# Moving the on-chip addresses of an encoder layer's tiles: large tiles to multiples of 1 KB, small tiles into two pools of their own

## The chip, the cores and the metric

The kernel runs on one core of one Trainium2 chip. The metric is the device time of one launch in microseconds (us), as the median of several runs. The engines are named as in the profile: PE is TensorE (PEld its weight load, the read of the stationary operand), DVE is VectorE, ACT is ScalarE, POOL is GpSimd, SP is SyncE. A tile is a piece of on-chip memory: 128 partitions, and in each partition a run of bytes that begins at the same address. When an address is given below, it is the byte address within a partition.

## The reference, cut to what matters

One encoder layer on 256 tokens of width 2048, everything in float32:

```
x = x + 0.5 * swiglu(rmsnorm(x, ffn1_norm), ffn1_w_gate, ffn1_w_up, ffn1_w_down)   # inner width 5632
h = rmsnorm(x, mix_norm)
proj  = h @ w_in                                    # pool | q | k | v | q_mem | three gates
gates = sigmoid(proj[..., c5:] + b_gate)
merged = gates_0 * (pooling_branch(u_pool, pool_w, pool_scale) @ w_up_pool)
       + gates_1 * (dilated_attention_branch(q, k, v, positions) @ w_up_attn)
       + gates_2 * (memory_branch(q_mem, rmsnorm(mem, mem_norm), w_mem_kv) @ w_up_mem)
x = x + merged @ w_out
x = x + 0.5 * swiglu(rmsnorm(x, ffn2_norm), ffn2_w_gate, ffn2_w_up, ffn2_w_down)
return rmsnorm(x, final_norm)
```

The weights are read once (the page counts 458 MB read from HBM), and nearly all the arithmetic is matrix products against them.

## The kernel before, in words

**Products.** Every float32 product is made of three float32r products: each operand is split into a high part (`wh`, `lhs[:, 0]`) and a low part (`wl`, `lhs[:, 1]`), and PE adds low times high, high times high and high times low (`gemm`, lines 495 to 522). The weights are the moving operand, 512 columns at a time; the activations are the stationary operand, 128 columns at a time. So a usual PE instruction streams 512 float32r numbers (2,048 bytes of each partition) from `wh`, `wl`, `sumsh` or `sumsl`, and has loaded 128 columns (512 bytes) from `lhs` or `seven`. The two feed-forward parts use a scheme of seven instead of eight block products for six of the eight row pairs (`pair_gemm`, lines 535 to 602).

**Path of a weight tile.** SP issues a 1 MB load of `wf`; ACT rounds it to `wh`; DVE subtracts to get `wl` (`split`, lines 424 to 431, called from `weights` and `pair_weights`); PE uses both. PE's results in PSUM are taken up by ACT and DVE (`finish`, lines 604 to 623). Where an activation has to be turned, PE does it with the 128 x 128 identity tile `ident` as an operand (`turn_steps`, lines 706 to 717).

**Tiles and pools.** All on-chip tiles come from one pool `sb`. Large ones share 23 places of 8 KB ("slot", line 395), 4 of 4 KB ("tmp", line 401) and 2 of 2 KB ("half", line 404). Small ones (`one`, `gains`, `small`, `rstd`, `ssq`, `pos_i`) take a few bytes, rounded up to 32, and `ident` takes 512 bytes. The pool lays its places one behind the other, in the order in which each is first used.

**Order.** The kernel first records all instructions, and a planner (`Plan`, lines 178 to 372) orders them by estimated durations and gives each tile one of its group's places. The planner knows places by number and not by address.

Of the kernel before, what the change touches and what calls it, by code (L numbers as in the profile page):

```python
# [9 lines left out]
F32 = mybir.dt.float32  # L10
F32R = mybir.dt.float32r
BF16 = mybir.dt.bfloat16
I32 = mybir.dt.int32
# [4 lines left out]
P = 128  # L18
S = 256
T = S // P  # L20
D = 2048
KB = D // P
DFF = 5632
CW = 512
NCH = D // CW
# [24 lines left out]
def turn_parts():  # L50

    from fractions import Fraction

    pi = Fraction(
        314159265358979323846264338327950288419716939937510582097494459230781640628620899,
        10 ** 80,
    )
    rest = 1 / (2 * pi)
    parts = []
    for bits in (14, 26, 38, 50, 62):  # L60
        n = int(rest * 2 ** bits)
        parts.append(float(n) / 2.0 ** bits)
        rest -= Fraction(n, 2 ** bits)
    return parts
# [317 lines left out]
@with_exitstack  # L382
def tile_encoder_layer(ctx: ExitStack, tc: tile.TileContext, a: dict, out: bass.AP):
    nc = Plan(tc)
    sb = nc.pool(ctx.enter_context(tc.tile_pool(name="sb", bufs=1)))
    ps = nc.pool(ctx.enter_context(tc.tile_pool(name="ps", bufs=1, space=bass.MemoryType.PSUM)))
    dr = nc.pool(ctx.enter_context(tc.tile_pool(name="dr", bufs=1, space=bass.MemoryType.DRAM)))
    count = [0]

    def nm(s):  # L390
        count[0] += 1
        return f"{s}{count[0]}"

    def slot(shape, dtype=F32, name="slot"):
        return sb.tile(shape, dtype, tag="slot", bufs=23, name=nm(name))
# [4 lines left out]
    def tmp(shape, name="tmp", dtype=F32):  # L400
        return sb.tile(shape, dtype, tag="tmp", bufs=4, name=nm(name))
# [2 lines left out]
        return sb.tile(shape, dtype, tag="half", bufs=2, name=nm(name))  # L404

    def small(shape, name="sm"):
        return sb.tile(shape, F32, tag="small", bufs=10, name=nm(name))

    def psum(i, shape, name="bank"):
        return ps.tile(shape, F32, tag=f"p{i}", bufs=1, name=nm(name))  # L410
# [212 lines left out]
                nc.scalar.activation(c, Q[q], AF.Copy)  # L623


    one = sb.tile([P, 1], F32, name="one")
    nc.vector.memset(one, 1.0)
    nc.scalar.activation(one, one, AF.Copy)

# [2 lines left out]
    idle_out = psum(7, [P, CW], "idle")  # L632
    for _ in range(WARM):
        nc.tensor.matmul(idle_out, idle_in[:, :P], idle_in, start=True, stop=True)
    gains = sb.tile([P, 4 * KB + 8], F32, name="gains")
    nc.sync.dma_start(out=gains, in_=a["gains"])
    g_ffn1, g_mix, g_mem, g_ffn2 = (gains[:, i * KB : (i + 1) * KB] for i in range(4))
    pool_scale = gains[:, 4 * KB :]

    ident = sb.tile([P, P], F32, name="ident")  # L640
    nc.gpsimd.memset(ident, 1.0)
    nc.gpsimd.affine_select(
        out=ident, in_=ident, pattern=[[-1, P]], base=0, channel_multiplier=1, compare_op=ALU.is_equal, fill=0.0
# [137 lines left out]
        nc.scalar.activation(junk, src, AF.Square, accum_out=ssq[:, t, n : n + 1])  # L781

    def rstd_tile(nt=T):
        return sb.tile([P, nt], F32, tag="rstd", bufs=4, name=nm("rstd"))

    def rstd_of(ssq, nt=T, r=None):

        if r is None:
            r = rstd_tile(nt)
        v, q = small([P, nt]), small([P, nt])  # L790
        nc.vector.reduce_sum(v, ssq, axis=AX.X)
        nc.vector.tensor_scalar(v, v, 1.0 / D, EPS, op0=ALU.mult, op1=ALU.add)
        nc.scalar.activation(q, v, AF.Sqrt)
        nc.vector.reciprocal(r, q)
        nc.vector.tensor_mul(q, r, r)
        nc.vector.tensor_mul(q, q, v)
        nc.vector.tensor_scalar(q, q, -0.5, 1.5, op0=ALU.mult, op1=ALU.add)
        nc.vector.tensor_mul(r, r, q)
        return r

    def late_rstd(ssq):
        r = rstd_tile()
        queue(lambda: rstd_of(ssq, r=r))
        return r

    def ssq_tile():
        return sb.tile([P, T, NCH], F32, tag="ssq", bufs=2, name=nm("ssq"))


    lhs1 = pair_tiles()  # L810
    ssq1 = ssq_tile()
    rstd1 = []
    xts = []
# [116 lines left out]

    def rope_pieces():
        freq = tmp([P, H], "freq")
        pos_i = sb.tile([P, T], I32, name="pos_i")
        pos = small([P, T], "pos")
        work = slot([P, 14, T * H], F32, "angle")
        hi_r = slot([P, T * H], F32R, "hi_r")
        whole = slot([P, 10, T * H], F32, "whole")
        ang, hi, lo, acc = work[:, 10], work[:, 11], work[:, 12], work[:, 13]
        prod = work[:, :10]

        def load():
            nc.sync.dma_start(out=freq, in_=a["freq"])
            nc.sync.dma_start(out=pos_i, in_=a["positions"])

        def angles():
            nc.vector.tensor_copy(pos, pos_i)
            for t in range(T):
                nc.vector.tensor_scalar(ang[:, t * H : (t + 1) * H], freq, pos[:, t : t + 1], None, op0=ALU.mult)
            nc.vector.tensor_copy(hi_r, ang)
            nc.vector.tensor_copy(hi, hi_r.bitcast(F32))  # L950
            nc.vector.tensor_sub(lo, ang, hi)
            for i, part in enumerate(turn_parts()):
                nc.vector.tensor_scalar(work[:, i], lo, part, None, op0=ALU.mult)
                nc.vector.tensor_scalar(work[:, 5 + i], hi, part, None, op0=ALU.mult)


        def within(m):
            nc.vector.tensor_scalar(whole, prod, m, -m, op0=ALU.add, op1=ALU.add)
            nc.vector.tensor_sub(prod, prod, whole)

        def wrap(x):
            nc.vector.tensor_scalar(whole[:, 0], x, ROUND, -ROUND, op0=ALU.add, op1=ALU.add)
            nc.vector.tensor_sub(x, x, whole[:, 0])

        def total():
            nc.vector.tensor_add(acc, work[:, 4], work[:, 9])
            wrap(acc)
            for i in (3, 8, 2, 7, 1, 6, 0, 5):
                nc.vector.tensor_add(acc, acc, work[:, i])
                wrap(acc)  # L970


        def tables():
            quarter = ang
            nc.vector.tensor_scalar_add(quarter, acc, 0.25)
            wrap(quarter)
            scale = float(np.float32(2 * np.pi))
            for t in range(T):
                c, s = quarter[:, t * H : (t + 1) * H], acc[:, t * H : (t + 1) * H]
                nc.scalar.activation(rope[:, t, 0, :H], c, AF.Sin, scale=scale)  # L980
                nc.scalar.activation(rope[:, t, 0, H:], c, AF.Sin, scale=scale)
                nc.scalar.activation(rope[:, t, 1, :H], s, AF.Sin, scale=-scale)
                nc.scalar.activation(rope[:, t, 1, H:], s, AF.Sin, scale=scale)

        return [load, angles, lambda: within(ROUND_FAR), lambda: within(ROUND), total, tables]
# [4 lines left out]
    def mem_pieces():  # L990

        ssq = ssq_tile()
        rows, columns = {}, {}

# [31 lines left out]

    lhs_mix = []
    ssq2 = ssq_tile()

    def after1(n, t, xs):  # L1030
# [31 lines left out]
    def mem_head(qT, kT, v, h, L):  # L1062
# [3 lines left out]
        def scores():  # L1066
            b = bank([P, T, S])
            for t in range(T):
                for db in range(2):
                    j = 2 * h + db  # L1070
                    for x, y in THREE:
                        nc.tensor.matmul(
                            b[:, t], qT[:, x, j, t * P : (t + 1) * P], kT[:, y, j],
                            start=db == 0 and x == 1, stop=db == 1 and y == 1,
                        )
            mx, den = small([P, T]), small([P, T])
            scale = 256 ** -0.5
            nc.vector.reduce_max(mx, b, axis=AX.X)
            nc.vector.tensor_scalar(mx, mx, -scale, None, op0=ALU.mult)
            p = half_tmp([P, T, S], F32, "pm")  # L1080
            for t in range(T):
                nc.scalar.activation(
                    p[:, t], b[:, t], AF.Exp, bias=mx[:, t : t + 1], scale=scale, accum_out=den[:, t : t + 1]
                )
            nc.vector.reciprocal(den, den)
            for t in range(T):
                nc.vector.tensor_scalar(p[:, t], p[:, t], den[:, t : t + 1], None, op0=ALU.mult)
            state["p"] = p
# [115 lines left out]
    def gated(i, n, lhs, w_up, first, beside=None):  # L1204
# [26 lines left out]
        queue(*(lambda t=t: merge(t) for t in range(T)), soon=True)  # L1231

    rope_work = rope_pieces()
    for n in range(NCH):
        for _ in range(2 if n < 3 else 0):
# [248 lines left out]
```

## Time and profile before

| | us |
|---|---|
| median of 3 runs (2306.33 to 2308.55) | 2307.55 |
| the profiled execution, its own time | 2307.88 |
| its span, first to last instruction in the trace | 2306.1 |
| PE busy | 2286.4 |
| DVE busy | 1871.0 |
| ACT busy | 1270.7 |

PE is busy for 99% of the span, and its granted clock is full (2.4 GHz) in nearly all of it. Since matmuls overlap each other in the pipeline, the busy time doesn't say how fast PE goes; the distance from one matmul's start to the next one's does. The feed-forward parts lie at about 0 to 760 us and 1600 to 2297 us, the branches between them. All program lines carry the helper's number L225, so groups are told apart by the names of the tiles.

### The profile page before, as it was taken

How to read it: one execution, taken by the hardware profiler on the slowest of the kernel's cores; microseconds unless marked ns; L12 is line 12 of the kernel's file. 1: busy time of each engine (PE TensorE's matmuls, PEld its weight loads, DVE VectorE, ACT ScalarE, POOL GpSimd, SP SyncE). 2: the span in 40 equal slices, each digit the busy share in tenths (PEclk: the TensorE clock that was granted, in tenths of full speed). 3: DMA queues.
4: the chain of work that ended last, by engine and by line, in shares of the span. 5: the costliest groups of instructions: out<-in, count | busy, mean ns of one | idle time of the engine just before them, and what ended most of it. 6: DMA issues, size and time to landing. Idle time of an engine off the chain costs nothing.

```text
span 2306.1 us, 26456 instructions
## 1 busy us (share of the span) xinstructions
PE 2286.4 (99%) x10211; PEld 1866.8 (81%) x10211; DVE 1871.0 (81%) x1805; ACT 1270.7 (55%) x1244; POOL 163.6 (7%) x221
## 2 busy tenths in 40 slices
PE   9999999999999999999999999999999999999998
PEld 6887888888887888888888888888888888888886
DVE  7999999999987675856677567876599999999995
ACT  8666666666666453633333554445466666666663
POOL 0011111111110000000000000000001111111110
PEclk9999999999999999999999999999999999999999
DMA  9578788877886453655455556656477878778893
GB/s 347 191 230 236 238 238 249 228 224 233 249 320 223 171 214 119 230 194 201 170 195 182 174 201 214 225 208 215 144 224 230 240 222 243 234 223 245 237 301 119
DMA packets 115822, 506.18 MB, mean 219 GB/s; under 512 B 13680, under 2 KB 13936, under 8 KB 84464
## 3 DMA queue, kind: packets, MB, share of 16 engines
q1 hardware_dynamic: 88416, 443.66, 54.8%
q0 software_dynamic: 26992, 59.78, 12.8%
q8 instruction: 80, 1.31, 0.2%
q10 hardware_dynamic: 288, 1.05, 0.1%
q14 instruction: 46, 0.38, 0.0%
HBM read 458.30 MB, written 46.14 MB: 219 GB/s over the span
## 4 chain that ended last, share of the span: by engine, by line
PE 56%; issue 35%; POOL 4%; DMA 2%; DVE 2%; ACT 1%; SPq 0%; POOLq 0%; DVEq 0%; ACTq 0%
PE acc L225 39%; PE q L225 12%; POOL x L225 4%; PE down L225 3%; PE bank L225 2%; DMA x<-y 1%; DVE wl L225 1%; DMA mem<-in_mem 1%; DMA wf<-in_ffn_w_up 0%; DMA xt<-in_memT 0%; ACT wh L225 0%; DVE sums L225 0%; DVE lhs L225 0%; SPq L225 0%; ACT junk L225 0%
## 5 line engine op out<-in xcount | busy, mean ns | idle before, releaser
L225 DVE TENSOR_TENSOR wl<-wf,wh 128x2048 fp32r<-128x2048 f32 (+2 forms) x419 | 885.0, 2126 | 162.3 <-ACT wh L225 121.3
L225 ACT ACTIVATE wh<-wf 128x2048 fp32r<-128x2048 f32 (+2 forms) x419 | 741.4, 1783 | 305.9 <-PE acc L225 108.8
L225 PE MATMUL acc<-wh,lhs 128*128 128x512 f32 x2688 | 842.0, 394 | 0.0
L225 PEld LDWEIGHTS acc<-wh,lhs 128*128 128x128 f32 x2688 | 498.0, 188 | 107.3
L225 PE MATMUL acc<-wl,lhs 128*128 128x512 f32 x1344 | 525.5, 392 | 0.4 <-DVE wl L225 0.4
L225 PE MATMUL down<-wh,lhs 128*128 128x512 f32 x1152 | 359.2, 391 | 0.0
L225 PE MATMUL q<-wh,seven 128*128 128x512 f32 x972 | 303.4, 393 | 4.0 <-DVE lhs L225 2.0
L225 ACT ACTIVATE sumsh<-sums 128x1024 fp32r<-128x1024 f32 x228 | 237.1, 1057 | 117.2 <-DVE sums L225 117.2
L225 PEld LDWEIGHTS acc<-wl,lhs 128*128 128x128 f32 x1344 | 252.6, 188 | 56.0 <-DVE wl L225 1.1
L225 PE MATMUL q<-sumsh,seven 128*128 128x512 f32 x912 | 274.5, 391 | 0.0
L225 DVE TENSOR_TENSOR sumsl<-sums,sumsh 128x2048 fp32r<-128x2048 f32 x114 | 260.5, 2285 | 15.3 <-ACT sumsh L225 15.0
L225 PEld LDWEIGHTS down<-wh,lhs 128*128 128x128 f32 x1152 | 216.3, 188 | 47.6
L225 PE MATMUL q<-wh,lhs 128*128 128x512 f32 x704 | 232.2, 411 | 1.0 <-ACT wh L225 1.0
L225 ACT ACTIVATE y<-down 128x512 f32<-128x512 f32 x144 | 86.4, 600 | 254.8 <-PE down L225 141.8
L225 PE MATMUL down<-wl,lhs 128*128 128x512 f32 x576 | 225.4, 391 | 0.0
L225 PEld LDWEIGHTS q<-wh,seven 128*128 128x128 f32 x972 | 182.3, 189 | 46.3 <-PE q L225 4.8
L225 POOL DMA_DIRECT2D x<-y x144 | 123.9, 860 | 1133.1 <-ACT y L225 1126.1
L225 PEld LDWEIGHTS q<-sumsh,seven 128*128 128x128 f32 x912 | 171.2, 188 | 37.4
L225 PE MATMUL q<-wl,seven 128*128 128x512 f32 x486 | 190.0, 392 | 0.0
L225 DVE TENSOR_TENSOR sums<-sums,wf 128x512 f32<-128x512 f32 x228 | 157.8, 692 | 7.7
L225 PE MATMUL q<-sumsl,seven 128*128 128x512 f32 x456 | 163.6, 391 | 0.0
L225 PEld LDWEIGHTS q<-wh,lhs 128*128 128x128 f32 x704 | 120.2, 189 | 32.4 <-ACT wh L225 2.5
(137 smaller groups left out, 1603.9 us busy)
## 6 DMA issues: line engine op xcount, KB each, us to landing
wf<-in_w_in SPq DMA_DIRECT2D x100, 1024.0 KB, 4.9
wf<-in_ffn_w_down SPq DMA_DIRECT2D x88, 1024.0 KB, 7.1
wf<-in_ffn_w_gate SPq DMA_DIRECT2D x175, 512.0 KB, 5.2
wf<-in_ffn_w_up SPq DMA_DIRECT2D x175, 512.0 KB, 6.7
x<-y POOLq DMA_DIRECT2D x144, 256.0 KB, 6.4
wf<-in_w_mem_kv SPq DMA_DIRECT2D x16, 1024.0 KB, 4.9
wf<-in_w_out SPq DMA_DIRECT2D x16, 1024.0 KB, 4.9
wf<-in_w_up_pool SPq DMA_DIRECT2D x8, 1024.0 KB, 4.8
```

The lines of the kernel that those rows point to most:

```text
L225: return getattr(getattr(self.nc, engine), name)(*map(real, args), **{k: real(v) for k, v in kw.items()})
```

## The change

The program that is built before and after has the same 16,160 instructions in the same order on each engine, with the same waits. What differs is where tiles lie. The small tiles go to a pool `sm` that is laid ahead of the large tiles, `ident` to a pool `end` behind them, and `one` is made 64 bytes long, which makes `sm` 896 bytes; together with 128 bytes of constants that precede it, the large tiles then begin at 17,408 = 17 x 1,024. The places behind it are 8, 4 and 2 KB long, so that all of them begin at multiples of 1 KB.

The addresses, as the allocator's table in each built program has them:

| tiles | before | mod 1,024 (mod 64) | after | mod 1,024 (mod 64) |
|---|---|---|---|---|
| 21 of the 23 slots, the 1st tmp place | 17,344 to 185,280 | 960 (0) | 17,408 to 185,344 | 0 (0) |
| the 2 half places | 193,504 and 195,552 | 992 (32) | 193,536 and 195,584 | 0 (0) |
| the other 2 slots | 197,600 and 205,792 | 992 (32) | 197,632 and 205,824 | 0 (0) |
| the other 3 tmp places | 213,984 to 222,176 | 992 (32) | 214,016 to 222,208 | 0 (0) |
| `rope` | 226,752 | 448 (0) | 226,304 | 0 (0) |
| `ident` | 16,544 | 160 (32) | 228,352 | 0 (0) |
| small tiles | 16,512; 17,056; 193,472; 226,272 to 226,720; 228,800 | multiples of 32 | 16,512 to 17,376 | multiples of 32 |

Before, a 32-byte small tile (`ssq`, at 193,472) lies between the slots and the half places, which is why all that follows it stands 32 bytes off the rest. Within a tile, PE's operands begin at multiples of 512 bytes, so the remainders of the table hold for them too.

```diff
-    sb = nc.pool(ctx.enter_context(tc.tile_pool(name="sb", bufs=1)))
+
+    sm = nc.pool(ctx.enter_context(tc.tile_pool(name="sm", bufs=1)))
+    sb = nc.pool(ctx.enter_context(tc.tile_pool(name="sb", bufs=1)))
+    end = nc.pool(ctx.enter_context(tc.tile_pool(name="end", bufs=1)))
...
     def small(shape, name="sm"):
-        return sb.tile(shape, F32, tag="small", bufs=10, name=nm(name))
+        return sm.tile(shape, F32, tag="small", bufs=10, name=nm(name))
...
-    one = sb.tile([P, 1], F32, name="one")
+    one = sm.tile([P, 16], F32, name="one")[:, :1]
...
-    gains = sb.tile([P, 4 * KB + 8], F32, name="gains")
+    gains = sm.tile([P, 4 * KB + 8], F32, name="gains")
...
-    ident = sb.tile([P, P], F32, name="ident")
+    ident = end.tile([P, P], F32, name="ident")
...
-        return sb.tile([P, nt], F32, tag="rstd", bufs=4, name=nm("rstd"))
+        return sm.tile([P, nt], F32, tag="rstd", bufs=4, name=nm("rstd"))
...
-        return sb.tile([P, T, NCH], F32, tag="ssq", bufs=2, name=nm("ssq"))
+        return sm.tile([P, T, NCH], F32, tag="ssq", bufs=2, name=nm("ssq"))
...
-        pos_i = sb.tile([P, T], I32, name="pos_i")
+        pos_i = sm.tile([P, T], I32, name="pos_i")
```

## Rows read from the trace of the kernel before

**Rows 1.** The page: busy us (share of span) and instructions by engine.

```profile
PE 2286.4 (99%) x10211; PEld 1866.8 (81%) x10211; DVE 1871.0 (81%) x1805; ACT 1270.7 (55%) x1244; POOL 163.6 (7%) x221
PEclk9999999999999999999999999999999999999999
```

**Rows 2.** The waits of PE: waiter <- releaser, us in total, times, longest.

```profile
PE q L225 <- ACT wh L225: 2.9, 3, 2.0
PE bank L225 <- DVE lhs L225: 2.7, 1, 2.7
PE q L225 <- DVE lhs L225: 2.0, 5, 0.8
```

**Rows 3.** Groups by shape, DVE and ACT: count | busy us, mean ns | idle before.

```profile
L225 DVE TENSOR_TENSOR wl<-wf,wh 128x2048 fp32r<-128x2048 f32 x301 | 685.8, 2287 | 158.8 <-ACT wh L225 117.9 <-PE acc L225 32.7 <-issue 7.1
L225 ACT ACTIVATE wh<-wf 128x2048 fp32r<-128x2048 f32 x301 | 573.6, 1912 | 280.4 <-PE acc L225 108.8 <-DMA wf<-in_w_in 91.5 <-DVE wl L225 19.9
```

**Rows 4.** Stretches: start:end length, busy by engine (count), clock, DMA share, GB/s.

```profile
1089.61:1095.05 5.44, 5.44 (x26) 4.50 (x24) 4.05 (x2) 2.55 (x2) 0.00 (x0) 1.00 0.63 193
1095.73:1101.33 5.60, 5.60 (x25) 4.50 (x24) 5.44 (x13) 1.38 (x2) 0.00 (x0) 1.00 0.83 310
1542.58:1548.02 5.44, 5.44 (x26) 4.37 (x25) 1.23 (x5) 2.91 (x4) 0.00 (x0) 1.00 0.00 0
1548.02:1553.62 5.60, 5.60 (x26) 4.51 (x24) 3.69 (x3) 2.48 (x2) 0.00 (x0) 1.00 0.55 189
934.65:937.37 2.72, 2.72 (x14) 2.25 (x12) 2.72 (x2) 2.72 (x2) 0.00 (x0) 1.00 0.44 69
937.37:940.15 2.78, 2.78 (x14) 2.25 (x12) 2.78 (x2) 2.76 (x3) 0.00 (x0) 1.00 0.77 318
940.15:942.93 2.78, 2.78 (x14) 2.25 (x12) 2.78 (x3) 0.73 (x1) 0.00 (x0) 1.00 0.04 15
942.93:945.65 2.72, 2.72 (x14) 2.25 (x12) 2.69 (x4) 2.37 (x3) 0.24 (x1) 1.00 0.80 250
```

**Rows 5.** PE in order of time: start us, length, instruction, count [idle before].

```profile
349.78 0.39 PE L225 MATMUL q<-wl,lhs 128*128 128x512 f32 x1
350.94 0.70 PE L225 MATMUL q<-wh,seven 128*128 128x512 f32 x2 [0.77 <-DVE lhs L225]
351.48 0.40 PE L225 MATMUL q<-wl,seven 128*128 128x512 f32 x1
351.71 0.62 PE L225 MATMUL q<-sumsh,seven 128*128 128x512 f32 x2
352.40 0.62 PE L225 MATMUL q<-sumsh,seven 128*128 128x512 f32 x2
353.10 0.62 PE L225 MATMUL q<-sumsh,seven 128*128 128x512 f32 x2
353.78 0.62 PE L225 MATMUL down<-wh,lhs 128*128 128x512 f32 x2
...
354.46 0.62 PE L225 MATMUL down<-wh,lhs 128*128 128x512 f32 x2
```

**Rows 6.** DVE ahead of the wait in rows 5, same columns.

```profile
335.52 0.69 DVE L225 TENSOR_TENSOR v<-q,gate 128x512 f32<-128x512 f32 x1 [3.75 <-DMA x<-y]
...
347.31 2.28 DVE L225 TENSOR_TENSOR wl<-wf,wh 128x2048 fp32r<-128x2048 f32 x1
...
350.11 0.68 DVE L225 TENSOR_TENSOR lhs<-bank,lhs 128x512 fp32r<-128x512 f32 x1
```

**Rows 7.** Stretches as in rows 4: the two feed-forward parts without their ends.

```profile
60.00:760.00 700.00, 695.81 (x3086) 565.79 (x3085) 639.05 (x554) 436.36 (x442) 73.91 (x94) 1.00 0.77 238
1640.00:2200.00 560.00, 559.42 (x2480) 456.10 (x2479) 514.78 (x421) 344.53 (x326) 55.90 (x65) 1.00 0.76 226
```

**Rows 8.** PE where the stretch from 937.37 (rows 4) ends, columns of rows 5.

```profile
939.70 0.61 PE L225 MATMUL acc<-wh,lhs 128*128 128x512 f32 x2
940.15 0.40 PE L225 MATMUL acc<-wl,lhs 128*128 128x512 f32 x1
```

## The prediction

> **What bounds the kernel now.** I read the page first: PE is busy 2286.4 of 2306.1 us at a full granted clock [rows 1]. The list of PE's waits then says who holds it up: nobody for long. The three longest waits that come from other engines add up to 7.6 us, over 9 occasions [rows 2]. So the time is the number of PE's instructions times the distance from one start to the next. The program has 10,211 matmuls as the trace counts them, 9,642 of which stream 512 columns of float32r. If an address matters, it must show as a longer distance, or it must shorten what feeds PE.
>
> The program and the trace have the same number of matmuls in the same order, so each start in the trace can be laid beside the addresses of its operands in the built program. Before the change 21 of 23 slots lie at multiples of 64 bytes, and two lie 32 bytes off such a multiple, together with three tmp places, the half places and `ident`. That gives two kinds of operand to compare within one execution: "on" (address divisible by 64) and "off" (32 over).
>
> **What the rows show.** Four pairs of neighbouring stretches do it [rows 4]. (a) From 1089.61 us on, 24 matmuls with both operands on take 5.44 us, which is 226.7 ns each. From 1095.73 on, the next 24 stream a weight tile that lies at 205,792 (off), and take 5.60 us, or 233.3 ns each. (b) In the product with w_out, the 24 matmuls up to 1548.02 have both operands on: 5.44 us. The 24 from there on have their stationary operand in the tile at 205,792 (off), and the moving one on: 5.60 us. (c) From 937.37 on only every third matmul (the one with `wl`) is off. Blocks of 12 take 2.72, then 2.78, 2.78, then 2.72 us as the off tile comes and goes. In the third of these blocks the DMA engines are at 4% and in the fourth at 80%, so it isn't the traffic. DVE's and ACT's instructions show nothing of the kind: the 301 long `wl` subtractions average 2,287 ns and the 301 roundings 1,912 ns [rows 3], and told apart by on and off, in classes of 27 and more, their medians lie within 1 ns of each other for DVE and within 4 ns for ACT.
>
> There is a second way to a longer distance, which the change doesn't touch. After any break PE needs some ten matmuls to fall back into its step. After the wait that ends at 350.94, on operands that are all on, the threes that start at 351.71, 352.40 and 353.10 take 0.69, 0.70 and 0.68 us, and from 353.78 on 0.68 [rows 5]. The same happens after each group of turns with `ident`.
>
> The Trainium skill has a rule that speaks against all this: "SBUF — State Buffer", section Specifications, gives lines of 16 bytes, with a cost for crossing lines. A start 32 bytes over is a whole number of such lines, so by that rule on and off cost the same and the sum below is nothing. The trace doesn't agree: 5.44 against 5.60 us [rows 4].
>
> **The change, part by part.** *Moving the off tiles to multiples of 64.* In the program 1,570 of the 9,642 wide matmuls read at least one off operand (1,186 the moving one, 376 the stationary one, 8 both). Two prices follow from the rows. In a run of 24 each costs 0.16 us / 24 = 7 ns. In the pattern of every third, a block with 4 costs 0.06 us, or 15 ns each, since its neighbours are slowed too. So the price of all is between 1,570 x 7 = 11 and 1,570 x 15 = 24 us. Laid out one by one, the 9,343 wide matmuls with a distance under 260 ns fall into four kinds. 3,976 are far (over 12 matmuls) from any off operand, turn or break: they average 226.7 ns, as in the 5.44 us of [rows 4]. 3,812 are within 12 behind an off operand alone: 230.5 ns, together 14.6 us over the step of 226.7. 986 are within 12 behind a break or a turn alone: 3.4 us over. 569 are behind both: 2.8 us over, of which 569 x 3.5 ns = 2.0 would be there for the break alone. What goes with the off operands is 14.6 + 0.8 = 15.4 us, inside the bounds of 11 and 24.
>
> *Moving the on tiles* from 960 to 0 mod 1,024. No row shows an operand of PE at a multiple of 128, so this is bounded. From above: it could be as bad as off, 8,072 x 6.6 ns = 53 us. From below: the step of 226.7 ns is at 2.4 GHz 544 cycles for 512 columns; if all of the excess went, 13.4 ns x 9,642 = 129 us. I take nothing, the value of the nearest rows: all that is known to matter is the remainder by 64, and that stays 0; the distances between on tiles stay the same as well.
>
> *Moving `ident`* from off to on. The 3.4 + 2.0 us behind breaks and turns could go with it if the turns lose their step because `ident` is off. I take 0 of it, since a plain wait leaves the same trail with no `ident` in sight [rows 5]. As a bound it is -5 us.
>
> *Small tiles, half places, tmp places:* read and written by DVE and ACT, whose times show no address [rows 3], and off PE's path: nothing. *DMA:* the rows that loads write now start at multiples of 1 KB. The engines are at 77% and 76% in the feed-forward parts [rows 7], so a few per cent either way stay hidden behind PE.
>
> *What is late next.* DVE is the nearest: 639 of 700 us, 91%, in the first feed-forward part [rows 7]. Most of the time it runs ahead and waits. But at each chunk's end (63 us apart, some 20 in all) it is tied to PE: it takes up PSUM banks from 335.52 on, works without a break, and frees at 350.79 the bank for which PE waits 0.77 us [rows 5, 6]. In those 15 us DVE's work is fixed, so what PE saves there, 15 us x 0.7% = 0.1 us, comes back as a longer wait. For the 5 boundaries that wait already [rows 2] that is 0.5 us; if all 20 came to wait, 2 us. I take 1.2.
>
> *Sum:* -15.4 + 1.2 = -14.2 us. The profiled execution took 2307.88 us, 0.3 more than the median of 2307.55. From the median: 2293.3 us, 0.6% faster.
>
> **The rivals.**
> *R1, the slowness isn't of the remainder.* The two off slots are also the two highest, at 197,600 and 205,792, above 192 KB (196,608), and no PE operand of 512 columns lies high and on, or low and off. If the height is what slows PE, the change doesn't do what it says, since they stay high (197,632 and 205,824): 2307.5 us. For it: the rows can't part the two. Against it: with one off matmul in three, the 11th and 12th matmul of a block (939.70 to 940.15) are back at 0.45 us for two while the tile is still in use [rows 8], which looks like two streams running in and out of phase, not like a slower memory. By the rule of 16-byte lines the time would be the same.
> *R2, a finer remainder matters too, to the good.* Then the on tiles gain as well. One ns on each of 8,072 is 8 us; if the 544 cycles came half-way to 512, PE would save 65 us, and DVE at 91% would stop it at some 5%. For it: nothing is known of 0 mod 128. Against it: one step for all 21 on slots, whatever shares the memory with them. Time: about 2250 us.
> *R3, slower through the loads.* All loads now write rows that start at the same remainder of 1 KB. If that made the packets of one load meet in the same place of the memory, DMA time would grow. PE feels it only when the share passes 1, that is from 1 / 0.77 = 1.30 times the present time on. At 1.33 times, the 1,260 us of the two feed-forward parts would grow by 2.4%: +30 us, 2323 us with the gain above counted. Against it: before, 22 large places already shared one remainder (960).
>
> **How the numbers follow.** The forecast has 80%: 15.4 us from a count over one execution whose instructions stay the same, with a known cost for the two kinds of matmul. Within it the time goes from 2307.5 - 15.4 - 5 = 2287 (with the trails behind turns) to 2307.5 - 11 + 2 = 2299. R1 has 11%, R2 5%, R3 4%. The forecast's own range of 2287 to 2299 covers eight in ten, and nothing need be added. A measurement of this kernel can tell about 0.2% (4.6 us, the line at 2302.9) from no change. All of the forecast and R2 lie under it: 85% faster; R1 is 11% the same; R3 is 4% slower.
>
> **What would show it.** In the profile after, the long `wl` group of DVE stays at 2,287 ns. Runs of 24 wide matmuls take 5.44 us everywhere, also in the stretches that answer to 1095.73, 1548.02 and 937.37 [rows 4]; the trail behind waits stays. PE's waits for `lhs` from DVE grow by 1 or 2 us. If those stretches still take 5.60 us, the height of the two slots is the cause (R1). If the clean stretches fall below 5.44, it is R2. If PE's waits for `wh` grow by tens of us with loads that land later, it is R3.

## The result

The changed kernel takes 2290.9 us (median of 4 runs, 2290.32 to 2293.08) against 2307.86 us before. The ratio is 0.9929, with a 95% interval of 0.9912 to 0.9946. The forecast was 2293.3 us, in a range of 2287 to 2299. The time came as forecast, but the property that the prediction named as the cause, the remainder by 64, is not the cause. The experiments below found the one that is.

The page of the kernel after, the lines that answer to [rows 1]:

```profile
PE 2267.9 (99%) x10211; PEld 1865.5 (81%) x10211; DVE 1870.2 (82%) x1805; ACT 1270.1 (55%) x1244; POOL 163.4 (7%) x221
PEclk9999999999999999999999999999999999999999
```

PE lost 18.5 us of busy time with the same number of instructions; DVE and ACT lost less than 1 us each. The stretches of the kernel after that answer to those of [rows 4] (start:end, length, busy by engine with counts, granted clock, DMA share, GB/s):

```profile
1079.63:1085.08 5.45, 5.45 (x26) 4.51 (x25) 4.20 (x2) 2.79 (x2) 0.00 (x0) 1.00 0.59 192
1085.76:1091.19 5.43, 5.43 (x25) 4.50 (x24) 5.27 (x13) 1.03 (x2) 0.00 (x0) 1.00 0.82 305
1535.87:1541.31 5.44, 5.44 (x25) 4.51 (x24) 3.66 (x3) 2.47 (x2) 0.00 (x0) 1.00 0.54 194
928.45:931.17 2.72, 2.72 (x14) 2.25 (x12) 2.72 (x2) 2.70 (x3) 0.00 (x0) 1.00 0.89 355
931.17:933.89 2.72, 2.72 (x14) 2.25 (x12) 2.72 (x3) 0.81 (x1) 0.00 (x0) 1.00 0.03 12
```

The second and third rows are the same 24 matmuls each that took 5.60 us before, and the last two are the blocks of 12 that took 2.78. They now go at the pace of the undisturbed ones, 226.7 ns a matmul. The two highest slots are still the highest (197,632 and 205,824), and the second and third rows read them, so the rival R1 (height) falls here already. The waits of PE after, against [rows 2]:

```profile
PE q L225 <- DVE lhs L225: 3.4, 6, 1.0
PE q L225 <- ACT wh L225: 3.2, 3, 1.9
PE bank L225 <- DVE lhs L225: 2.6, 1, 2.6
```

PE's waits for `lhs` from DVE grew from 2.0 to 3.4 us.

**Where the 16.7 us between the two profiled executions lie** (spans of 2306.1 and 2289.4 us, matmuls laid side by side one for one; a distance is that from a matmul's start to the next one's):

| | before | after | difference |
|---|---|---|---|
| wide matmuls with a distance under 260 ns, their time over 226.7 ns each | 20.9 | 5.9 | -15.0 |
| breaks (260 ns and more), their time over 226.7 ns | 36.9 | 35.5 | -1.4 |
| ... of it, matmuls at half clock behind the first 5.5 us | 3.2 | 0.2 | -3.0 |
| ... of it, the rest, PE's waits for others among it | 33.7 | 35.3 | +1.6 |
| other matmuls, start and end | 62.8 | 62.5 | -0.3 |

The line of the half clock isn't the change's doing. In the profiled execution before, the granted clock fell to the lower level (1.2 of 2.4 GHz) for 16 matmuls behind two long waits, which cost 3 us. A second profile of the same kernel (label before_again) doesn't have it. The first 60 us and 15 us around the longest wait, of the kernel before:

```profile
0.00:60.00 60.00, 55.78 (x224) 42.25 (x225) 43.11 (x73) 48.73 (x77) 5.17 (x14) 0.97 0.87 334
690.00:705.00 15.00, 12.30 (x51) 9.56 (x51) 8.24 (x19) 11.68 (x27) 3.26 (x6) 0.89 0.96 374
```

and of its second profile:

```profile
0.00:60.00 60.00, 55.84 (x232) 42.69 (x232) 44.87 (x74) 50.49 (x78) 5.14 (x14) 1.00 0.88 334
690.00:705.00 15.00, 12.50 (x60) 9.90 (x59) 9.18 (x22) 12.03 (x28) 3.31 (x7) 1.00 0.88 341
```

The clock (0.97 and 0.89 against 1.00) and the count of matmuls (224 and 51 against 232 and 60) show it. That execution took 2304.2 us. The slower matmuls are in both profiles in the same size: 20.9 us over the step of 226.7 ns in each. So 13 to 15 us are the change's, and up to 3 us depend on which executions are compared.

### The profile page after: what moved, and what is told of

The parts are those of the page before. It is cut to its first block, busy times and chain, and to the rows that moved or that the text cites. A ratio compares the mean times of both kernels' runs of the same rounds, so it can differ in the third digit from the quotient of the medians.

```text
span 2289.4 us, 26456 instructions
## 1 busy us (share of the span) xinstructions
PE 2267.9 (99%) x10211; PEld 1865.5 (81%) x10211; DVE 1870.2 (82%) x1805; ACT 1270.1 (55%) x1244; POOL 163.4 (7%) x221
## 4 chain that ended last, share of the span: by engine, by line
PE 56%; issue 35%; POOL 4%; DMA 2%; DVE 2%; ACT 1%; SPq 0%; POOLq 0%; DVEq 0%; ACTq 0%
PE acc L225 39%; PE q L225 12%; POOL x L225 4%; PE down L225 3%; PE bank L225 2%; DMA x<-y 1%; DVE wl L225 1%; DMA mem<-in_mem 1%; DMA wf<-in_ffn_w_up 0%; DMA xt<-in_memT 0%; ACT wh L225 0%; DVE sums L225 0%; DVE lhs L225 0%; SPq L225 0%; ACT junk L225 0%
```

## The experiments

In what follows a "difference" is the start address of the moving operand less that of the stationary one. Each run's own time is compared with runs of the kernel before on the same chip.

**1. Only the high tiles put on (ssq64).**

```diff
-        return sb.tile([P, T, NCH], F32, tag="ssq", bufs=2, name=nm("ssq"))
+        return sb.tile([P, 2 * T, NCH], F32, tag="ssq", bufs=2, name=nm("ssq"))[:, :T]
```

> The kernel before with one edit: the small tile that lay between the slots takes 64 bytes instead of 32. All 21 on slots, the small tiles and ident stay where they were, at 960 mod 1,024 (ident 32 over a multiple of 64); the two high slots, the half and tmp places move by 32 bytes to multiples of 64. All 9,642 wide matmuls then read on operands. Theory (the remainder by 64 decides): about 2291 us, the whole gain of the change, with runs of 24 matmuls at 5.44 us everywhere. Rival R1 (the height of the two slots): 2307.5 us, nothing gained. Rival R2 (a finer remainder, such as 128 or 1,024, gave part of the gain): between 2293 and 2307 us.

Measured: 2309.7 us, ratio 1.0014 (1.0005 to 1.0024). So it is not faster but a trace slower. The theory and R2 are off; R1's "nothing gained" comes close, but R1 had fallen with the result. Every wide matmul reads operands at multiples of 64 here, so the remainder by 64 is not what matters. The stretches that answer to the first four of [rows 4], the clean one before the third left out:

```profile
1092.61:1098.05 5.44, 5.44 (x25) 4.50 (x24) 4.02 (x2) 2.80 (x2) 0.00 (x0) 1.00 0.51 193
1098.73:1104.24 5.51, 5.51 (x25) 4.51 (x24) 5.35 (x13) 0.98 (x2) 0.00 (x0) 1.00 0.81 302
1551.23:1556.83 5.60, 5.60 (x25) 4.51 (x24) 3.69 (x3) 2.49 (x2) 0.00 (x0) 1.00 0.53 189
```

In the second the weight tile lies at 0 mod 1,024 and the stationary one at 960: both at multiples of 64, with a difference of 64, and still slow. In the third the difference is -64, and the time is the 5.60 us of before.

**2. Two low tiles put off (low_off).** The places of the pool get a pad ahead of the seventh slot and one behind the eighth:

```diff
+                    key, pad = f"{tag or name}_{place}", lambda n: real.tile([P, 8], F32, tag=n, bufs=1, name=n)
+                    if key == "slot_6" and "before" not in pads:
+                        pads["before"] = pad("pad_before")
...
+                    if key == "slot_7" and "behind" not in pads:
+                        pads["behind"] = pad("pad_behind")
```

> The changed kernel with two 32-byte pads around two low slots, at 66,592 and 74,784, so that these two alone lie 32 bytes off a multiple of 64, and the two high slots (above 192 KB) are on. 1,575 wide matmuls read an off operand, against 1,570 in the kernel before. Theory (remainder by 64): the slowness comes back, 2291 + 15 to 16 = about 2306 us. Rival R1 (height of the slots): 2291 us or less than before by as much, since no high slot changes its kind from the changed kernel in a way that matters to it; if it was the height together with the remainder, also 2291 us.

Measured: 2324.99 us, ratio 1.0076 (1.006 to 1.0093), slower than any expectation. The pads move all that lies behind them too, so there are three kinds of slot: six at 0 mod 1,024, two at 32 and fifteen at 64. Only 4,487 of the 9,642 wide matmuls have a difference of 0 mod 256, against 8,080 before. The two stretches of 24 that answer to 1089.61 and 1095.73 of [rows 4]:

```profile
1095.91:1101.49 5.58, 5.58 (x25) 4.51 (x24) 3.94 (x2) 3.25 (x2) 0.00 (x0) 1.00 0.52 188
1102.19:1107.64 5.45, 5.45 (x25) 4.50 (x24) 5.29 (x13) 0.57 (x1) 0.00 (x0) 1.00 0.81 299
```

They have changed places. The first reads, in 14 of its 24 matmuls, a weight tile at 33,792 (0 mod 64) against a stationary one at 115,776 (0 mod 64), with a difference of 192 mod 256, and is slow. The second reads the high weight tiles at 205,888 and 197,696 against 107,584, with a difference of 0, and is fast. So high tiles are fast here and low ones slow: the height of the two slots isn't the cause.

**3. All large tiles put off (all_off).**

```diff
-    one = sm.tile([P, 16], F32, name="one")[:, :1]
+    one = sm.tile([P, 24], F32, name="one")[:, :1]
```

> The changed kernel with the first small tile 32 bytes longer, so that every large tile lies 32 bytes off a multiple of 64. All 9,642 wide matmuls read both operands off. Theory (each off operand costs by itself): 6.6 ns on each, 64 us, so about 2355 us, and more if two off operands cost more than one. Rival (only the difference between the remainders of the moving and the stationary operand costs, and these are equal here): 2291 us. Rival R1 (height): 2291 us.

Measured: 2293.48 us, ratio 0.9942 (0.9927 to 0.9957). With every wide matmul off in both operands, the kernel is as fast as the changed one. The rival named there, that only the difference costs, is the one that holds. The answers to [rows 4]:

```profile
1081.54:1086.98 5.44, 5.44 (x26) 4.50 (x24) 4.19 (x2) 2.64 (x2) 0.00 (x0) 1.00 0.60 193
1087.66:1093.10 5.44, 5.44 (x26) 4.50 (x24) 5.28 (x13) 1.09 (x2) 0.00 (x0) 1.00 0.83 304
1537.77:1543.21 5.44, 5.44 (x26) 4.50 (x24) 3.67 (x3) 2.48 (x2) 0.00 (x0) 1.00 0.56 194
```

**4. Matmuls alone (steps).** Two resident tiles that begin at multiples of 1 KB; each run of 36 reads them at chosen offsets:

```
for i in range(36):
    w = so + (i % 2) * 512 bytes
    matmul(bank, still[:, w : w + 128], moving[:, mo : mo + 512], ...)
```

> A kernel of its own with nothing but matmuls on two resident tiles that begin at multiples of 1 KB; it computes nothing of the reference and writes a copy of x. Runs of 36 matmuls, 512 columns of float32r, with the start of the moving and of the stationary operand moved by a chosen number of bytes: (0,0), (32,0), (0,32), (32,32), (64,0), (0,64), (64,64), (128,0), (256,0), (16,0), (0,16), (16,16), (48,0), (0,48), (8,0), (4,0), (0,4), (4,4), with (0,0) between the groups; then four runs with 256 columns, and seven with bf16. Theory (remainder by 64): 226.7 ns a matmul at 0, 64, 128 and 256; 233 ns at 32 of either operand; 4 to 48 slow as well, nothing said on how much. Rival (difference of remainders): (32,32), (16,16) and (4,4) at 226.7 ns. Rival R2 (finer remainders): (64,0), (0,64) or (128,0) slower than (0,0). bf16: open, no theory speaks of it.

24 matmuls out of each run; in order, the offsets (moving, stationary) in bytes are (0,0), (32,0), (0,32), (32,32), (64,0), (0,64), (64,64), (128,0), (256,0), (16,16), (4,4), then 512 columns of bf16 at (0,0) and (32,0):

```profile
27.18:32.62 5.44, 5.44 (x25) 4.50 (x24) 0.00 (x0) 0.00 (x0) 0.00 (x0) 1.00 0.02 3
35.41:41.01 5.60, 5.60 (x25) 4.50 (x24) 0.00 (x0) 0.00 (x0) 0.00 (x0) 1.00 0.00 0
43.81:49.41 5.60, 5.60 (x26) 4.51 (x24) 0.00 (x0) 0.00 (x0) 0.00 (x0) 1.00 0.00 0
52.16:57.60 5.44, 5.44 (x25) 4.50 (x24) 0.00 (x0) 0.00 (x0) 0.00 (x0) 1.00 0.00 0
68.56:74.05 5.49, 5.49 (x25) 4.51 (x24) 0.00 (x0) 0.00 (x0) 0.00 (x0) 1.00 0.00 0
76.84:82.44 5.60, 5.60 (x25) 4.49 (x24) 0.00 (x0) 0.00 (x0) 0.00 (x0) 1.00 0.00 0
85.19:90.63 5.44, 5.44 (x25) 4.51 (x24) 0.00 (x0) 0.00 (x0) 0.00 (x0) 1.00 0.01 3
93.41:98.97 5.56, 5.56 (x25) 4.51 (x24) 0.00 (x0) 0.00 (x0) 0.00 (x0) 1.00 0.00 0
101.76:107.20 5.44, 5.44 (x25) 4.50 (x24) 0.00 (x0) 0.00 (x0) 0.00 (x0) 1.00 0.00 0
134.85:140.37 5.52, 5.52 (x25) 4.50 (x24) 0.00 (x0) 0.00 (x0) 0.00 (x0) 1.00 0.00 0
193.46:199.17 5.71, 5.71 (x26) 4.54 (x24) 0.00 (x0) 0.00 (x0) 0.00 (x0) 1.00 0.00 0
227.13:232.31 5.18, 5.18 (x25) 2.35 (x24) 0.00 (x0) 0.00 (x0) 0.00 (x0) 1.00 0.00 0
234.90:240.08 5.18, 5.18 (x25) 2.35 (x24) 0.00 (x0) 0.00 (x0) 0.00 (x0) 1.00 0.00 0
```

No other engine works and next to nothing is moved by DMA (at most 3 GB/s), and the two paces of [rows 4] are there to the digit. (32,32) and (64,64) are as fast as (0,0), and (32,0), (0,32), (64,0), (0,64) and (128,0) are slow. The price belongs to a difference, and 256 is free again. The difference has a sign: (0,64) is -64, which is 192 mod 256, and takes 5.60 us, while (64,0) takes 5.49. Below 32 bytes the start itself counts as well: (16,16) takes 5.52 us and (4,4) 5.71, both with a difference of 0. With bf16 no offset that was tried changes anything.

**5. The period inside the kernel (low_256).** Like experiment 2, with the first pad alone, of 256 bytes in place of 32.

> The changed kernel with one pad of 256 bytes ahead of the seventh slot, so that six slots lie at 0 mod 1,024 and 17 at 256. 4,174 of the 9,642 wide matmuls then read operands that differ by 256 mod 512, the others operands that differ by 0. After the first four runs the theory is that the difference of the two operands' starts costs, by its remainder, and that 256 is as good as 0 (the matmul kernel showed 226.67 ns at 256): about 2291 us. Rival (only a common remainder by 1,024, or by 512, is free): 4,174 matmuls at up to 6.6 ns and their neighbours, 2310 to 2330 us.

Measured: 2291.88 us, ratio 0.9933 (0.9918 to 0.9948). Six slots at 0 and seventeen at 256 mod 1,024 cost nothing; a difference of 256 is as good as 0 in the kernel too.

**6. The period and the price of each difference (steps_fine).**

> The kernel of matmuls alone again, with the moving operand's start moved by 32 to 512 bytes in steps of 32, then the stationary operand's by 32 to 256, then both at 0 with the two stationary blocks that take turns 0, 512, 1,024, 256, 128, 64 and 32 bytes apart, then 256 columns with the moving operand moved by 0 to 256 in steps of 32. It computes nothing of the reference. Theory (difference mod 256): 226.7 ns at 0, 256 and 512, over 228 at all others, the same at d and d + 256; two stationary blocks 64 apart disturb like a difference of 64. If some difference lies under 226.7 ns, a faster layout than both kernels exists. If 288 and 32 differ, the period is longer than 256.

18 matmuls out of each run, with the moving operand moved by 32, 64, 96, 128, 160, 192, 224, 256 and 288 bytes, then with both at 0 and the two stationary blocks 256, 128 and 64 bytes apart:

```profile
27.30:31.50 4.20, 4.20 (x19) 3.37 (x18) 0.00 (x0) 0.00 (x0) 0.00 (x0) 1.00 0.01 4
34.26:38.38 4.12, 4.12 (x20) 3.38 (x19) 0.00 (x0) 0.00 (x0) 0.00 (x0) 1.00 0.00 0
41.18:45.38 4.20, 4.20 (x20) 3.38 (x18) 0.00 (x0) 0.00 (x0) 0.00 (x0) 1.00 0.00 0
48.18:52.38 4.20, 4.20 (x19) 3.38 (x18) 0.00 (x0) 0.00 (x0) 0.00 (x0) 1.00 0.00 0
55.19:59.41 4.22, 4.22 (x20) 3.39 (x19) 0.00 (x0) 0.00 (x0) 0.00 (x0) 1.00 0.02 4
62.21:66.41 4.20, 4.20 (x20) 3.37 (x18) 0.00 (x0) 0.00 (x0) 0.00 (x0) 1.00 0.00 0
69.20:73.40 4.20, 4.20 (x19) 3.38 (x18) 0.00 (x0) 0.00 (x0) 0.00 (x0) 1.00 0.00 0
76.16:80.24 4.08, 4.08 (x19) 3.38 (x18) 0.00 (x0) 0.00 (x0) 0.00 (x0) 1.00 0.00 0
83.03:87.23 4.20, 4.20 (x19) 3.37 (x18) 0.00 (x0) 0.00 (x0) 0.00 (x0) 1.00 0.00 0
221.59:225.67 4.08, 4.08 (x19) 3.38 (x18) 0.00 (x0) 0.00 (x0) 0.00 (x0) 1.00 0.00 0
228.46:232.66 4.20, 4.20 (x19) 3.42 (x18) 0.00 (x0) 0.00 (x0) 0.00 (x0) 1.00 0.00 0
235.43:239.57 4.14, 4.14 (x20) 3.38 (x18) 0.00 (x0) 0.00 (x0) 0.00 (x0) 1.00 0.02 4
```

4.08 us is 226.7 ns a matmul, 4.12 is 228.9, 4.20 is 233.3 and 4.22 is 234.3. Of the multiples of 32, only a difference of 0 mod 256 is free, 64 is cheap, and the rest costs 6.6 to 7.6 ns. From 256 on the row repeats; the run to 512 bytes gives the same prices again. The low price of 64 is that of an even run. In the kernel of experiment 1, in the blocks of 12 where only every third matmul has a difference of 64, a block takes 2.78 us, as at 32 before the change, and all wide matmuls together lie 22.2 us over the step against 20.9. None of the differences tried is faster than 0, so among these there is no better layout for matmuls of 512 columns than one remainder for all, which the changed kernel has.

**7. The two kernels once more (before_again, after_again).**

> The kernel before once more, for a second profile: how much of the 16.9 us lies in things that differ from execution to execution, such as the stretches at half the granted clock behind the long waits near 15 and 698 us. All theories: about 2307 us, and 5.60 us for the 24 matmuls that answer to 1095.73.

> The changed kernel once more, timed on the same chip as the others here: 2291 us, and a second profile for the same purpose. All theories agree.

Measured: 2304.2 us in one execution of the kernel before, and 2292.91 us for the changed one, ratio 0.9935 (0.9919 to 0.9952). The second profile of the kernel before supplied the rows on the clock above, and its 24 matmuls take 5.60 us again. The second profile after has 10 matmuls at half clock behind the first 5.5 us (2.0 us), and its wide matmuls lie 5.7 us over the step against 5.9 in the first.

**8. One edit alone (ssq_apart).** The kernel before, with the tile that lay between the slots moved away:

```diff
+    end = nc.pool(ctx.enter_context(tc.tile_pool(name="end", bufs=1)))
...
-        return sb.tile([P, T, NCH], F32, tag="ssq", bufs=2, name=nm("ssq"))
+        return end.tile([P, T, NCH], F32, tag="ssq", bufs=2, name=nm("ssq"))
```

> The kernel before with one edit: the 32-byte tile that lay between the slots goes to a pool of its own behind the large tiles. Every slot, half and tmp place then lies at 960 mod 1,024, the small tiles and ident stay ahead of them, nothing lies at a multiple of 1 KB, and the two operands of every wide matmul differ by 0 mod 256. Theory (the difference mod 256 decides): about 2291 us, the whole gain from this one edit. Rival (multiples of 128, 256 or 1,024 have a part in the gain, or ident's place has): between 2293 and 2307 us.

Measured: 2294.29 us, ratio 0.9953 (0.9937 to 0.997). The time doesn't part the theory from its rival: it lies 3 us over the theory's 2291 and just inside the rival's 2293 to 2307, and the interval overlaps those of the changed kernel (0.9912 to 0.9946 and 0.9919 to 0.9952). The trace does, as far as PE's pace goes. The stretches that answer to 1095.73 and 1548.02 of [rows 4]:

```profile
1086.80:1092.24 5.44, 5.44 (x26) 4.50 (x24) 5.28 (x13) 0.96 (x2) 0.00 (x0) 1.00 0.85 306
1536.91:1542.35 5.44, 5.44 (x25) 4.51 (x24) 3.66 (x3) 2.47 (x2) 0.00 (x0) 1.00 0.57 194
```

No large tile lies at a multiple of 1 KB here, or of 128, and `ident` stays off. The wide matmuls' time over the step is 5.7 us, as in the kernel after (5.9). In the profiled execution, 1.6 us are 8 matmuls at half clock. So this edit alone brings PE's whole gain; whether the 4 to 5 us between its ratio and those of the changed kernel are more than noise, these runs don't tell.

## Why the prediction was right, and where it was not

*What bounds the kernel.* Right: of the 16.7 us between the two profiles, 15.0 lie in PE's distance from start to start while it runs without a break; the clock and the waits make up the rest.

*The off tiles.* The sum held: 15.4 us forecast, 15.0 us measured between the two profiles. The reason given for it did not. The step that failed is the sentence that all that is known to matter is the remainder by 64. What matters is the difference of the two operands' starts mod 256: 960 against 992 is 32 one way round and 224 the other, and every pair of an off and an on operand in the kernel before has one of the two (1,186 and 376 matmuls). The rows couldn't tell the two readings apart, because off nearly always met on: of 1,570 matmuls with an off operand, 8 had two. That the tiles differ, and not that they are off, should have stood among the rivals. It was not there, and was first written down, after the result, as a rival in experiments 3 and 4, where it won. That the time came out right is in this part luck: the change brings all differences to 0 as well as all remainders. In experiments 1 to 3, where the two come apart, the recorded theory missed by 19, 19 and 62 us. One reading of the rows was loose: in pair (a), 16 of the 24 matmuls stream the tile at 205,792 and 8 the one at 197,600; both are off, so the price stands.

*The on tiles.* Taken as 0, and 0 measured: 226.7 ns before and after. But the bound of 53 us from above and the rival R2 rested on a property that plays no part: with all large tiles at 0, at 32 or at 960 mod 1,024, or at 0 and 256 mixed, the step is the same.

*`ident`.* Taken as 0, and 0 measured: the wide matmuls' time over the step, by then the trails behind turns and breaks, is 5.9 us after, with `ident` on, and 5.7 us in experiment 8, where it stays off.

*DVE as the next limit.* 1.2 us forecast; the breaks without the clock's part grew by 1.6 us, and PE's waits for `lhs` from DVE from 2.0 to 3.4 us (from 1.9 to 3.1 in the second profiles). So the size fits. That PE's gain is the reason isn't shown: in experiment 1, where PE gained nothing, these waits are 4.7 us.

*The clock.* Not in the sum. In the two profiled executions the half clock makes 3.0 of the 16.7 us, which is more than what lies between the forecast of -14.2 and -16.7 us. How much of the medians' -17.0 us is the clock's is open, since only single executions have a trace.

*The Trainium skill.* "SBUF — State Buffer", section Specifications, with its lines of 16 bytes, would have had no price for offsets of 32. The trace has one: 5.60 against 5.44 us [rows 4]. Of starts inside such a line, (4,4) takes 5.71 us, so a start off the line does cost as well. But (16,16) starts on a line and takes 5.52 us, so the lines alone don't give the prices.

*R1 and R3.* R1 fell with the result, and experiment 2 shows the same. Of R3 nothing was seen: no wait of PE for a load appears among its waits, its waits for `wh` went from 2.9 to 3.2 us, and the 19 us that low_off lost lie in the matmuls themselves, 39.8 us over the step against 20.9.

What stays open is why a difference costs. One guess is that the read of the moving operand and the weight load, which fetches the next stationary operand meanwhile, get in each other's way. No run here shows the two reads themselves, so this is not shown.

## What to carry to other kernels

Where float32r products of 512 columns bound a kernel, keep the start addresses of moving and stationary operands equal mod 256 bytes. Let no small tile lie between large ones in a pool, or give small tiles a pool of their own: 32 bytes in the wrong place cost 0.5 to 0.7% here, and the three kinds of remainder of experiment 2 cost 1.4% against experiment 3 on the same chip. And when a trace shows that one kind of tile is slow, ask what it meets, not only what it is: list the pairs that occur, and doubt any cause for which the other pair never occurs.

## What the runs showed of the hardware that was not expected

- A matmul of 512 float32r columns takes 226.7 ns at a difference of 0 mod 256 between its operands' starts, 228.9 ns at 64, and 233.3 to 234.3 ns at the other multiples of 32. With bf16 it takes 215.8 ns at all offsets tried.
- With 256 columns the order is another one. 18 matmuls with the moving operand moved by 0, 32, 192 and 256 bytes:

```profile
248.11:250.27 2.16, 2.16 (x20) 2.16 (x19) 0.00 (x0) 0.00 (x0) 0.00 (x0) 1.00 0.00 0
251.70:253.82 2.12, 2.12 (x21) 2.12 (x19) 0.00 (x0) 0.00 (x0) 0.00 (x0) 1.00 0.00 0
269.43:271.47 2.04, 2.04 (x21) 2.04 (x20) 0.00 (x0) 0.00 (x0) 0.00 (x0) 1.00 0.00 0
276.43:278.59 2.16, 2.16 (x21) 2.16 (x20) 0.00 (x0) 0.00 (x0) 0.00 (x0) 1.00 0.00 0
```

  At 0 each takes 120 ns, and at 192 it takes 113.3, the fastest of the multiples of 32 up to 256. A difference of 256 is as 0 here too.
- After a break or a change of difference, PE takes up to ten matmuls to come back to its step. Behind the wait that ends at 350.94 in the kernel before, and behind the same one after, the distances are 233, 236, 224, 231, 236, 228, 233, 231 (230 after), then 227 ns; in the kernel of matmuls alone many runs end their trail with 236, 228, 233, 231 as well, but some have a shorter one. Between runs of bf16 at different offsets there is none: the distances stay at 215 and 216 ns.
